# A hybrid GLA and S5 decoder block on one core: half of the S5 rotation on ScalarE, and the late products in another order

## The chip, the cores and the metric

The kernel runs on one core of one Trainium2 chip. The metric is the device time of one execution in microseconds (us), the median of three runs. TensorE (PE) multiplies matrices, VectorE (DVE) and ScalarE (ACT) work on elements, GpSimd (POOL) and SyncE (SP) issue most transfers. Each engine has one queue and works through it in order; semaphores hold an instruction until what it needs is there.

## The reference

One layer on 512 tokens plus 16 meta tokens of width 1024. After a norm, one wide product gives q, k, v, the attention gate r, the S5 input u and two mixing gates z. Attention and S5 run side by side:

```python
proj = rmsnorm(h, g_mix_pre) @ w_in            # q k v r a_low u z_gla z_ssm
o = gla_chunked(q, k, v, log_a)
o = rmsnorm(o, gla_norm_g) * silu(r)
y_gla = o @ w_o_gla
y_s = s5_ssm(u, ...)                            # complex diagonal state, 64 groups of 64 states
glu = gelu(y_s) @ w_glu + b_glu
y_ssm = glu[..., :D] * sigmoid(glu[..., D:])
mixed = sigmoid(z_gla) * y_gla + sigmoid(z_ssm) * y_ssm
h = h + rmsnorm(mixed @ w_out)
h = h + rmsnorm(square(relu(rmsnorm(h) @ w_ff1)) @ w_ff2)
```

In S5 each state is `x_t = L x_(t-1) + B u_t`, `y_t = Re(C x_t) + D u_t` with complex L, B and C.

## The kernel before

**Weights and slots.** Every large product is made with float32 split in two halves: `whi` is the rounded weight, `wlo` the rest, and 24 matmuls per 128 output columns (8 steps of k, three passes: whi with xh, whi with xl, wlo with xh) make one *slot*. For each slot SP loads `wraw` (512 KB), ScalarE makes `whi` (`split_hi`, L161), VectorE makes `wlo` (`split_w_lo`, L176). Each of the three has three buffers, and `slot()` fetches two slots ahead. The list `dense` holds the slots in the order in which PE runs them; `slot()` takes the next.

**What stands between the slots.** The S5 part goes through 8 blocks of 8 groups. In each block, five slots are run with the block's work between them: `turns` (rotation table E by `erot`, loads of U), `kernels` (small matmuls "M,BA" and the row `krow`), the previous block's `output`, `scan`, and the next block's `tables` (M2 and M1). In the first four blocks the slots are the attention's v, k, q and one gate product; `Head` does the attention itself, one block behind for its outputs.

**The late slots**, counted from 0 over the whole list: slots 30 to 33 are gate products z0 to z3, 34 to 41 the attention gate products r0 to r7 (`r_slot`), then z5, o0, o1, o2, z6, o3, o4, z7, o5, o6, o7 (42 to 52), where z is a mixing gate (`gate_slot`) and o an attention output product (`o_slot`). Block 5 has the slots 35 to 39, block 6 the slots 40 to 44, block 7 the slots 45 to 49. An r slot has ScalarE's sigmoid of the product, VectorE's two multiplications (by the product, by the normed attention output `ro`), ScalarE's rounding into `ogh` and VectorE's rest into `ogl`. A z slot has only ScalarE's sigmoid behind it, an o slot only one multiplication by the kept or reloaded gate tile `zt`, which has 4 buffers. All o slots need all of `ogh` and `ogl`.

**The scan.** Real parts lie in partitions 0 to 63, imaginary parts in 64 to 127. `scan` multiplies M1 with U ("U,M"), rotates the result by E, scans along time, and rotates back. A rotation is one product with E's real part over all partitions and, in `turn`, two products with E's imaginary part over 64 partitions each, that read one half of the partitions and write the other, then a sum.

**Order.** A scheduler orders each engine's instructions in the region of the S5 blocks from the program's order and its own estimates; only PE's matmuls keep program order. Instructions keep the order that it found, on every run.

Of the kernel before, what the change touches and what calls it, by code (L numbers as in the profile page):

```python
# [11 lines left out]
AF = mybir.ActivationFunctionType  # L12
# [4 lines left out]
P = 128  # L17
D = 1024
KT = D // P
SEQ = 512  # L20
# [16 lines left out]
T8 = 8  # L37
# [12 lines left out]
def hybrid_block(ctx: ExitStack, tc: tile.TileContext, io, out: bass.AP):  # L50
    nc = tc.nc
    V, S, G = nc.vector, nc.scalar, nc.gpsimd
# [27 lines left out]
    def mk(pool, shape, dt=F32, tag=None, **kw):  # L80
        count[0] += 1
        name = f"{tag or 'x'}_{count[0]}"
        size = 1
        for n in shape[1:]:
            size *= n
        if pool not in lined or size % LINE == 0:
            return pool.tile(shape, dt, tag=tag or name, name=name, **kw)
        t = pool.tile([shape[0], -(-size // LINE) * LINE], dt, tag=tag or name, name=name, **kw)[:, :size]
        if len(shape) == 2:
            return t  # L90
        dims = " ".join("abcd"[: len(shape) - 1])
        return t.rearrange(f"p ({dims}) -> p {dims}", **dict(zip("abcd", shape[1:])))
# [29 lines left out]
    sgn = mk(cst, [P, 1], tag="sgn")  # L122
# [197 lines left out]
    V, S = InOrder(nc.vector), InOrder(nc.scalar)  # L320
# [107 lines left out]
    V, S = nc.vector, nc.scalar  # L428
# [3 lines left out]
    ps = bank()  # L432
# [56 lines left out]
    zg = mk(dr, [KT, P, SEQ], tag="zgd")  # L489
# [35 lines left out]
    def gate_slot(c0, m, dst, tile_of=None):  # L525

        def go(w):
            ps = bank("mm")
            feat_tile(w, xh, xl, 0, SEQ, ps)
            t = tile_of() if tile_of else mk(po_, [P, SEQ], tag="zt", bufs=4)  # L530
            S.activation(by_phase(t), phases(ps), AF.Sigmoid)
            if tile_of:
                nc.gpsimd.dma_start(dst[m], t)
            else:
                kept[m] = t

        dense.append((cols("w_in", c0 + m * P), go))
# [11 lines left out]
    Lr = mk(p5, [P, 9, GRP], tag="Lr")  # L549
    Li = mk(p5, [P, 9, GRP], tag="Li")  # L550
    CA = mk(p5, [P, GRP, HG], tag="CA")
    CB = mk(p5, [P, GRP, HG], tag="CB")
# [5 lines left out]
    behind_norm.__enter__()  # L558
    V.tensor_reduce(i16, ident.rearrange("p (b h) -> p h b", h=HG), axis=mybir.AxisListType.X, op=ALU.add)

# [52 lines left out]
    with tc.issue_after(loaded.ins):  # L613
        for i, name in enumerate(("b_re", "b_im")):
            nc.sync.dma_start(bn[:, i], io[name][0])
        for i, name in enumerate(("c_re", "c_im")):
            src = io[name][0].rearrange("(t g) h n -> (g h) t n", g=GB)
# [119 lines left out]
    def c_rows():  # L737
        for t0 in range(0, NBLK, 4):
            for src, dst, sg_ in ((cnat, CA, True), (cnatx, CB, False)):
                yield  # L740
                ps = bank()
                for t in range(4):
                    PE.transpose(ps[:, t * P : (t + 1) * P], src[:, t0 + t].rearrange("p a n -> p (a n)"), ident)
                d = dst[:, t0 * GB : (t0 + 4) * GB, :].rearrange("p g h -> p (g h)")
                V.tensor_scalar_mul(d, ps, sgn if sg_ else -1.0)

    def b_bar():

# [69 lines left out]
    b5 = pool("b5", stack=sb5, side="right")  # L818
# [154 lines left out]
    class Block:  # L973
# [3 lines left out]
            self.blk = blk  # L977
            self.gs = slice(blk * GB, (blk + 1) * GB)

        def table(self, dst, n, a_, b_, g0):  # L980
            gg = slice(self.blk * GB + g0, self.blk * GB + g0 + 4)
            sh = [P, 4, n, HG]
            d = dst[:, g0 : g0 + 4]
            ta = mk(b5, [P, 4, 9, HG], tag="mta")[:, :, :n]
            lrb = Lr[:, :n, gg].rearrange("p l g -> p g l").unsqueeze(3).to_broadcast(sh)
            lib = Li[:, :n, gg].rearrange("p l g -> p g l").unsqueeze(3).to_broadcast(sh)
            V.tensor_mul(d, a_[:, gg].unsqueeze(2).to_broadcast(sh), lrb)
            V.tensor_mul(ta, b_[:, gg].unsqueeze(2).to_broadcast(sh), lib)
            V.tensor_add(d, d, ta)

        def loads(self, queue=nc.sync):

            self.B = mk(b5, [P, GB, 2, NST_N], tag="B")
# [5 lines left out]
        def tables(self):  # L999

            M1 = self.M1 = mk(b5, [P, GB, 2, NST_N], tag="M1", bufs=1)
            self.M2 = mk(b5, [P, GB, 9, HG], tag="M2", bufs=2)
            B, (lr, li) = self.B, (self.lam[:, i].unsqueeze(2).to_broadcast([P, GB, 2, NST_N]) for i in range(2))
            for g0 in (0, 4):
                self.table(self.M2, 9, CA, CB, g0)
                yield
            V.tensor_mul(M1, B, lr)
            yield
            V.tensor_mul(B, B, li)
            V.tensor_sub(M1[:, :, 0], M1[:, :, 0], B[:, :, 1])  # L1010
            V.tensor_add(M1[:, :, 1], M1[:, :, 1], B[:, :, 0])
            yield
# [26 lines left out]
        def scan(self):  # L1039

            M3 = self.M3 = mk(b5, [P, GB, P], tag="M3", bufs=1)
            for sp in range(T8):
                s = T8 - 1 - sp
                nc.sync.dma_start(M3[sp * HG : (sp + 1) * HG], kpad[self.gs].rearrange("g h l -> h g l")[:, :, 112 - 16 * s : 240 - 16 * s])
            U, E = self.U, self.E
            v, vs = (mk(b5, [P, GB, NST], tag=t, bufs=1) for t in ("v", "vs"))

            def turn(src, gg):

                V.tensor_mul(vs[:64, gg], src[64:], E[64:, 1, gg])  # L1050
                V.tensor_mul(vs[64:, gg], src[:64], E[:64, 1, gg])  # L1051

            for g0 in range(0, GB, 4):
                ps = bank()
                pv = ps[:, : 4 * NST].rearrange("p (g c) -> p g c", g=4)
                for g in range(4):
                    PE.matmul(pv[:, g], self.M1[:, g0 + g].rearrange("p c n -> p (c n)"), U[:, g0 + g, :NST], start=True, stop=True)
                gg = slice(g0, g0 + 4)
                V.tensor_mul(v[:, gg], pv, E[:, 0, gg])
                turn(pv, gg)  # L1060
            V.tensor_sub(v, v, vs)
            flat = v.rearrange("p g c -> p (g c)")
            V.tensor_tensor_scan(flat, d0.rearrange("p g c -> p (g c)"), flat, 0.0, op0=ALU.mult, op1=ALU.add)  # L1063
            X = self.X = mk(b5, [P, GB, NST], tag="X", bufs=1)
            V.tensor_mul(X, v, E[:, 0])
            turn(v, slice(0, GB))
            V.tensor_add(X, X, vs)

        def output(self):

# [2 lines left out]
            for j in range(4):  # L1073
                for part in range(2):
                    for e in range(2):
                        g = 4 * e + j
                        if part:
                            a, b = self.X[:, g, 1:], self.M2[:, g, 1:9, :].rearrange("p l h -> p (l h)")
                        else:
# [30 lines left out]
    def r_slot(m):  # L1110
        def go(w):
            ps = bank("mm")
            feat_tile(w, xh, xl, 0, SEQ, ps)
            o = mk(po_, [P, SEQ], tag="ro", bufs=2)
            nc.sync.dma_start(o, og_dram[m])
            sg_ = mk(po_, [P, SEQ], tag="rs", bufs=2)
            S.activation(sg_, ps, AF.Sigmoid)
            V.tensor_mul(sg_, sg_, ps)
            V.tensor_mul(sg_, sg_, o)  # L1119
            split_hi(ogh[:, m], sg_)  # L1120
            V.tensor_sub(ogl[:, m], sg_, f32(ogh)[:, m])  # L1121

        dense.append((cols("w_in", C_R + m * P), go))

    def o_slot(m):
        def go(w):
            ps = bank("mm")
            feat_tile(w, ogh, ogl, 0, SEQ, ps)
            if m in kept:
                zt = kept.pop(m)  # L1130
            else:
                zt = mk(po_, [P, SEQ], tag="zt", bufs=4)
                nc.sync.dma_start(zt, zg[m])
            V.tensor_mul(by_phase(zt), by_phase(zt), phases(ps))
            nc.gpsimd.dma_start(td[m], zt)

        dense.append((cols("w_o_gla", m * P), go))
# [5 lines left out]
        gate_slot(C_ZS, 4 + h, zs, early_tile)  # L1143
    for m in range(4):
        gate_slot(C_ZG, m, zg, early_tile)
    for m in range(KT):
        r_slot(m)
    for kind, m in (("z", 5), ("o", 0), ("o", 1), ("o", 2), ("z", 6), ("o", 3), ("o", 4), ("z", 7), ("o", 5), ("o", 6), ("o", 7)):
        if kind == "o":
            o_slot(m)  # L1150
        else:
            gate_slot(C_ZG, m, zg)
    blocks[0].loads(nc.gpsimd)
    first = blocks[0].tables()
    for _ in range(4):
# [2 lines left out]
    for b, blk in enumerate(blocks):  # L1158
# [30 lines left out]
        if b == HEADS:  # L1189
# [3 lines left out]
            po_ = pool("po", stack=so, padded=True)  # L1193
# [39 lines left out]
    for c in range(0, D, 256):  # L1233
        ss_ = []
        for i, w in enumerate(load_w(wg[:, D + c : D + c + 256])):
            m = c // P + i
            ps = bank("mm")
# [3 lines left out]
            zt = mk(pgl, [P, SEQ], tag="zi", bufs=2)  # L1241
# [110 lines left out]
    f = mk(pff, [P, MF, SEQ], tag="f")  # L1352
# [44 lines left out]
    for m in range(EARLY, MF):  # L1397
        ps = bank("mm")
# [12 lines left out]
    po_ = pool("pout", side="right", padded=True)  # L1411
# [139 lines left out]
```

## Time and profile before

| | |
|---|---|
| time, median of 3 (lowest to highest) | 911.29 us (910.85 to 911.82) |
| the profiled execution: its time, its span | 912.54 us, 910.8 us |
| DVE busy | 668.6 us, 1182 instructions |
| ACT busy | 403.1 us, 656 instructions |
| S5 blocks 0 to 7 in the trace | from about 113 to 430 us |
| PE's part of the chain that ended last | 85% |

In the timeline a row is one instruction with its start and its duration; the brackets say how long its engine was idle before it and what ended that. An instruction's record overlaps the next one's by some hundredths. In the table by stretches, each engine's column is the time in which it was busy in that stretch, and PEclk is the clock granted to PE, 1.00 being full.

### The profile page before, as it was taken

The page shows a single profiled execution, that of the slowest core. Times are in us where ns is not written, and L with a number is a line of the kernel's source. Part 1 is how long each engine was busy: PE and PEld are TensorE (multiplying, and loading weights), DVE is VectorE, ACT ScalarE, POOL GpSimd, SP SyncE. Part 2 cuts the span into 40 slices and gives each one's busy share as a digit, 9 for nine tenths or more (in the row PEclk, how much of TensorE's full clock was granted, in tenths as well). Part 3 has the DMA queues.
Part 4 walks back from the last instruction along what each step waited for, and adds up shares of the span by engine and source line. Part 5 has one row for each costly group of instructions (what it writes and reads, how often), then busy time and mean ns, then how long its engine had stood idle before and what let it go on. Part 6 is the DMA issues. An engine that isn't in the chain of part 4 may idle for free.

```text
span 910.8 us, 13359 instructions
## 1 busy us (share of the span) xinstructions
PE 885.9 (97%) x4924; PEld 752.6 (83%) x4924; DVE 668.6 (73%) x1182; ACT 403.1 (44%) x656; POOL 92.1 (10%) x165
## 2 busy tenths in 40 slices
PE   8999999999999998699999999999999999999996
PEld 6998899898988787488888888988888888888885
DVE  7899788968787689845544676466866668688786
ACT  6363446556553433222422554333322236665763
POOL 1222100010101201012100000011111110000001
PEclk9999999999999999799999999999999999999999
DMA  7835855555445464747845683369898967856564
GB/s 222 215 110 172 230 137 161 138 139 157 111 149 160 131 146 130 198 124 213 266 144 154 198 214 110 132 199 346 291 336 289 342 238 232 294 190 191 178 208 140
DMA packets 175740, 176.13 MB, mean 193 GB/s; under 512 B 22917, under 2 KB 137673, under 8 KB 175674
## 3 DMA queue, kind: packets, MB, share of 16 engines
q1 hardware_dynamic: 158872, 117.89, 46.1%
q0 software_dynamic: 15632, 53.44, 16.8%
q10 hardware_dynamic: 1170, 3.94, 1.2%
q8 instruction: 39, 0.64, 0.3%
q14 instruction: 27, 0.22, 0.1%
HBM read 139.81 MB, written 35.42 MB: 192 GB/s over the span
## 4 chain that ended last, share of the span: by engine, by line
PE 85%; DVE 9%; DMA 2%; issue 2%; ACT 2%; SPq 0%; DVEq 0%; ACTq 0%
PE mm L60 62%; PE sm L60 20%; PE sm L65 2%; DMA wraw<-in_w_in_dram 1%; DVE wlo L176 1%; DVE mta L236 1%; DVE rs L1119 0%; DVE vs L1050 0%; DVE epb L237 0%; DVE vs L1051 0%; DVE v L1063 0%; DVE b L484 0%; PE mm L65 0%; DVE ogl L1121 0%; DVE mn L482 0%
## 5 line engine op out<-in xcount | busy, mean ns | idle before, releaser
L161 ACT ACTIVATE whi<-wraw 128x1024 fp32r<-128x1024 f32 x101 | 106.9, 1059 | 223.3 <-PE mm L60 196.4
L176 DVE TENSOR_TENSOR wlo<-wraw,whi 128x1024 fp32r<-128x1024 f32 x101 | 123.3, 1222 | 91.2 <-ACT whi L161 91.0
L60 PE MATMUL mm<-xh,whi 128*128 128x512 f32 (+2 forms) x544 | 183.1, 337 | 0.5 <-ACT xh L78 0.5
L60 PE MATMUL mm<-xh,wlo 128*128 128x512 f32 (+2 forms) x544 | 179.6, 330 | 2.8 <-DVE wlo L176 2.7
L60 PE MATMUL mm<-xl,whi 128*128 128x512 f32 (+2 forms) x544 | 179.1, 329 | 0.7 <-DVE xl L78 0.7
L60 PEld LDWEIGHTS mm<-xh,wlo 128*128 128x128 f32 x544 | 103.1, 189 | 12.7 <-DVE wlo L176 3.1
L60 PEld LDWEIGHTS mm<-xh,whi 128*128 128x128 f32 x544 | 103.1, 190 | 11.6 <-issue 1.4
L60 PEld LDWEIGHTS mm<-xl,whi 128*128 128x128 f32 x544 | 103.1, 190 | 9.6 <-DVE xl L78 1.1
L60 PE MATMUL mm<-hh,whi 128*128 128x512 f32 (+1 forms) x280 | 104.0, 371 | 0.0
L60 PE MATMUL mm<-hl,whi 128*128 128x512 f32 (+1 forms) x280 | 103.8, 371 | 0.0
L60 PE MATMUL mm<-hh,wlo 128*128 128x512 f32 (+1 forms) x280 | 103.8, 371 | 0.0
L1428 DVE TENSOR_TENSOR wlo<-wraw,whi 128x1024 fp32r<-128x1024 f32 x56 | 68.4, 1223 | 21.5 <-ACT whi L1424 21.5
L60 PE MATMUL sm<-wlo,fh 128*128 128x512 f32 x192 | 74.8, 390 | 0.0
L60 PE MATMUL sm<-whi,fl 128*128 128x512 f32 x192 | 74.7, 389 | 0.0
L60 PE MATMUL sm<-whi,fh 128*128 128x512 f32 x192 | 74.7, 389 | 0.0
L1424 ACT ACTIVATE whi<-wraw 128x1024 fp32r<-128x1024 f32 x56 | 58.7, 1049 | 18.5 <-PE mm L60 11.7
L60 PEld LDWEIGHTS mm<-hl,whi 128*128 128x128 f32 x280 | 52.7, 188 | 9.1
L60 PEld LDWEIGHTS mm<-hh,whi 128*128 128x128 f32 x280 | 52.7, 188 | 9.1
L60 PEld LDWEIGHTS mm<-hh,wlo 128*128 128x128 f32 x280 | 52.7, 188 | 9.0
L60 PE MATMUL mm<-gh,whi 128*128 128x512 f32 x128 | 49.8, 389 | 0.0
L60 PE MATMUL mm<-gl,whi 128*128 128x512 f32 x128 | 49.8, 389 | 0.0
L60 PE MATMUL mm<-gh,wlo 128*128 128x512 f32 x128 | 49.8, 389 | 0.0
(424 smaller groups left out, 1590.5 us busy)
## 6 DMA issues: line engine op xcount, KB each, us to landing
wraw<-in_w_ff_dram SPq DMA_DIRECT2D x56, 512.0 KB
wraw<-in_w_in_dram SPq DMA_DIRECT2D x48, 512.0 KB
w2raw<-in_w_ff_dram POOLq DMA_DIRECT2D x16, 1024.0 KB, 8.5
t2d<-w2t POOLq DMA_DIRECT2D x16, 1024.0 KB, 6.0
wraw<-t2d SPq DMA_DIRECT2D x32, 512.0 KB
wraw<-in_w_glu_dram SPq DMA_DIRECT2D x16, 512.0 KB
M<-kpad SPq DMA_DIRECT2D x64, 64.0 KB
wraw<-in_w_o_gla_dram SPq DMA_DIRECT2D x8, 512.0 KB
```

What stands on the lines that cost most here:

```text
L60: ins = nc.tensor.matmul(*args, **kw)
L65: ins = nc.tensor.transpose(*args, **kw)
L161: S.activation(dst, src, AF.Copy, scale=scale)
L176: V.tensor_sub(lo, raw, f32(hi))
L236: V.tensor_mul(ta, E[:, :, :, 1 : m + 1], br)
L1424: halved = S.activation(bh, raw, AF.Copy)
L1428: V.tensor_sub(bl, raw, f32(bh))
```

## The change

Three edits.

1. **Rotation.** `turn` becomes `exchanged`: ScalarE copies the lower partitions to the upper and the other way round (four copies of 64x260 out of PSUM and two of 64x520 per block), and VectorE then multiplies `vs` once by E's imaginary part over all 128 partitions. Signs move from one sum to the other.
2. **Tables.** M2's part for power 0 is a copy by ScalarE. The rest is one VectorE product over all 8 groups (128x1024) and two products and two sums over 4 groups (128x512), where there were three instructions of 128x576 for each half. The scaling of CA and CB (four instructions in `c_rows`) goes from VectorE to ScalarE.
3. **Slots.** The late slots run in the order r0, r1, z5, r2, r3, z6, r4, r5, r6, r7, z7, o0 to o7. `zt` has 6 buffers.

```diff
@@ gate_slot, o_slot @@
-            zt = mk(po_, [P, SEQ], tag="zt", bufs=4)
+            zt = mk(po_, [P, SEQ], tag="zt", bufs=6)
@@ c_rows @@
-                V.tensor_scalar_mul(d, ps, sgn if sg_ else -1.0)
+                S.activation(d, ps, AF.Copy, scale=sgn if sg_ else -1.0)
@@ Block.tables (table is removed) @@
-            V.tensor_mul(d, a_[:, gg].unsqueeze(2).to_broadcast(sh), lrb)
-            V.tensor_mul(ta, b_[:, gg].unsqueeze(2).to_broadcast(sh), lib)
-            V.tensor_add(d, d, ta)
...
+            S.copy(self.M2[:, :, 0], CA[:, self.gs])
...
+            V.tensor_mul(self.M2[:, :, 1:], ca, lrb)
             for g0 in (0, 4):
-                self.table(self.M2, 9, CA, CB, g0)
+                gg = slice(g0, g0 + 4)
+                ta = mk(b5, [P, 4, T8, HG], tag="mta")
+                V.tensor_mul(ta, cb[:, gg], lib[:, gg])
+                V.tensor_add(self.M2[:, gg, 1:], self.M2[:, gg, 1:], ta)
                 yield
@@ Block.scan @@
-            def turn(src, gg):
-
-                V.tensor_mul(vs[:64, gg], src[64:], E[64:, 1, gg])
-                V.tensor_mul(vs[64:, gg], src[:64], E[:64, 1, gg])
+            def exchanged(src, gg):
+
+                S.copy(vs[:64, gg], src[64:])
+                S.copy(vs[64:, gg], src[:64])
...
                 V.tensor_mul(v[:, gg], pv, E[:, 0, gg])
-                turn(pv, gg)
-            V.tensor_sub(v, v, vs)
+                exchanged(pv, gg)
+            V.tensor_mul(vs, vs, E[:, 1])
+            V.tensor_add(v, v, vs)
...
+            exchanged(v, slice(0, GB))
             V.tensor_mul(X, v, E[:, 0])
-            turn(v, slice(0, GB))
-            V.tensor_add(X, X, vs)
+            V.tensor_mul(vs, vs, E[:, 1])
+            V.tensor_sub(X, X, vs)
@@ the list of slots @@
-    for m in range(KT):
-        r_slot(m)
-    for kind, m in (("z", 5), ("o", 0), ("o", 1), ("o", 2), ("z", 6), ("o", 3), ("o", 4), ("z", 7), ("o", 5), ("o", 6), ("o", 7)):
...
+    for kind in ("r0", "r1", "z5", "r2", "r3", "z6", "r4", "r5", "r6", "r7", "z7", *(f"o{m}" for m in range(KT))):
...
```

The order of instructions shows what slot 44 waits for. On VectorE, between the last rotation of block 6 and the low half for slot 44, the program before has block 7's rotation table (mta, epb, E), its table M1 (M, B), and then the low half of o1 (`wlo_4233`):

```order
L236 TENSOR_TENSOR mta_4375<-E_4352 128x512
L237 TENSOR_TENSOR epb_4376<-E_4352 128x512
L238 TENSOR_TENSOR E_4352<-mta_4375,epb_4376 128x8x32
L239 TENSOR_TENSOR E_4352<-mta_4375,epb_4376 128x8x32
L1007 TENSOR_TENSOR M_752_4223<-B_4218,lam_4219 128x1024
L1009 TENSOR_TENSOR B_4218<-B_4218,lam_4219 128x1024
L1010 TENSOR_TENSOR M_752_4223<-M_752_4223,B_4218 128x8x64
L1011 TENSOR_TENSOR M_752_4223<-M_752_4223,B_4218 128x8x64
L176 TENSOR_TENSOR wlo_4233<-wraw_4229,whi_4231 128x1024
```

The program of the change has, at the same place, the product of r7 (`rs_4307`) among the same rows, and the low half of z7 (`wlo_4236`) at their end:

```order
L236 TENSOR_TENSOR mta_4385<-E_4362 128x512
L1117 TENSOR_TENSOR rs_4307<-rs_4307,mm_4280 128x512
L237 TENSOR_TENSOR epb_4386<-E_4362 128x512
L238 TENSOR_TENSOR E_4362<-mta_4385,epb_4386 128x8x32
L239 TENSOR_TENSOR E_4362<-mta_4385,epb_4386 128x8x32
L1004 TENSOR_TENSOR M_750_4225<-B_4220,lam_4221 128x1024
L1006 TENSOR_TENSOR B_4220<-B_4220,lam_4221 128x1024
L1007 TENSOR_TENSOR M_750_4225<-M_750_4225,B_4220 128x8x64
L1008 TENSOR_TENSOR M_750_4225<-M_750_4225,B_4220 128x8x64
L176 TENSOR_TENSOR wlo_4236<-wraw_4232,whi_4234 128x1024
L1118 TENSOR_TENSOR rs_4265<-rs_4265,ro_4263 128x512
```

So slot 44's low half has kept its place behind block 7's tables, and one product has joined the rows ahead of it. On ScalarE, at the same place, the program before has the sigmoid of r7 (`rs_4178`), the high half of o0, the roundings of r6 and r7, the sigmoid of z5 (`zt`), block 7's copies d and E and the high half of o1 (`whi_4231`):

```order
L1117 ACTIVATE rs_4178<-mm_4151 128x512
L161 ACTIVATE whi_4147<-wraw_4145 128x1024
L161 ACTIVATE ogh_3657<-rs_4102 128x512
L161 ACTIVATE ogh_3657<-rs_4178 128x512
L531 ACTIVATE zt_4260<-mm_4235 128x512
L1016 COPY d_217_1237<-prm_489 128x8x64
L1018 COPY E_4352<-E_88_491 128x16x9
L161 ACTIVATE whi_4231<-wraw_4229 128x1024
```

The program of the change has the sigmoid of r6 (`rs_4265`), the two exchanging copies of the scanned state (`vs` from `v`), d and E, the sigmoid of r7 (`rs_4307`) and the high half of z7 (`whi_4234`):

```order
L1116 ACTIVATE rs_4265<-mm_4238 128x512
L1047 COPY vs_4194<-v_4193 64x520
L1048 COPY vs_4194<-v_4193 64x520
L1013 COPY d_217_1237<-prm_489 128x8x64
L1015 COPY E_4362<-E_88_491 128x16x9
L1116 ACTIVATE rs_4307<-mm_4280 128x512
L161 ACTIVATE whi_4234<-wraw_4232 128x1024
```

Slot 44's high half has moved behind the sigmoid of slot 43, where before it stood behind the sigmoid of slot 42 only.

More of the change, by code (lines that the diff above doesn't have):

```diff
@@ L529, in go @@
             feat_tile(w, xh, xl, 0, SEQ, ps)
-            t = tile_of() if tile_of else mk(po_, [P, SEQ], tag="zt", bufs=4)
+            t = tile_of() if tile_of else mk(po_, [P, SEQ], tag="zt", bufs=6)
             S.activation(by_phase(t), phases(ps), AF.Sigmoid)
@@ L978, in __init__ @@
             self.gs = slice(blk * GB, (blk + 1) * GB)
[L980 to L987, printed above, removed]
-            V.tensor_mul(ta, b_[:, gg].unsqueeze(2).to_broadcast(sh), lib)
-            V.tensor_add(d, d, ta)
         def loads(self, queue=nc.sync):
@@ L1003, in tables @@
             B, (lr, li) = self.B, (self.lam[:, i].unsqueeze(2).to_broadcast([P, GB, 2, NST_N]) for i in range(2))
+            sh = [P, GB, T8, HG]
+            S.copy(self.M2[:, :, 0], CA[:, self.gs])
+            lrb, lib = (L[:, 1:, self.gs].rearrange("p l g -> p g l").unsqueeze(3).to_broadcast(sh) for L in (Lr, Li))
+            ca, cb = (C[:, self.gs].unsqueeze(2).to_broadcast(sh) for C in (CA, CB))
+            V.tensor_mul(self.M2[:, :, 1:], ca, lrb)
             for g0 in (0, 4):
-                self.table(self.M2, 9, CA, CB, g0)
+                gg = slice(g0, g0 + 4)
+                ta = mk(b5, [P, 4, T8, HG], tag="mta")
+                V.tensor_mul(ta, cb[:, gg], lib[:, gg])
+                V.tensor_add(self.M2[:, gg, 1:], self.M2[:, gg, 1:], ta)
                 yield
@@ L1145, in hybrid_block @@
         gate_slot(C_ZG, m, zg, early_tile)
-    for m in range(KT):
-        r_slot(m)
-    for kind, m in (("z", 5), ("o", 0), ("o", 1), ("o", 2), ("z", 6), ("o", 3), ("o", 4), ("z", 7), ("o", 5), ("o", 6), ("o", 7)):
-        if kind == "o":
-            o_slot(m)
+    for kind in ("r0", "r1", "z5", "r2", "r3", "z6", "r4", "r5", "r6", "r7", "z7", *(f"o{m}" for m in range(KT))):
+        m = int(kind[1])
+        if kind[0] == "z":
+            gate_slot(C_ZG, m, zg)
         else:
-            gate_slot(C_ZG, m, zg)
+            (r_slot if kind[0] == "r" else o_slot)(m)
     blocks[0].loads(nc.gpsimd)
```

## The prediction

> **What bounds the kernel now.** I read the page's busy shares first, then what PE waited for, then the stretches around the waits, then the rows at the waits.
>
> ```profile
> PE 885.9 (97%) x4924; PEld 752.6 (83%) x4924; DVE 668.6 (73%) x1182; ACT 403.1 (44%) x656; POOL 92.1 (10%) x165
> PE mm L60 <- DVE wlo L176: 8.2, 2, 5.5
> PE mm L60 <- ACT whi L161: 2.6, 1, 2.6
> PE sm L65 <- DVE CA L745: 1.6, 1, 1.6
> PE sm L65 <- ACT on L961: 0.5, 1, 0.5
> 340.00:360.00 20.00, 18.15 (x127) 14.78 (x125) 19.79 (x37) 7.72 (x13) 2.98 (x5) 1.00 0.50 137
> 360.00:380.00 20.00, 12.78 (x48) 9.86 (x48) 19.48 (x35) 5.99 (x8) 0.00 (x0) 0.85 0.78 182
> 380.00:400.00 20.00, 18.35 (x106) 14.72 (x107) 6.37 (x9) 1.92 (x4) 4.11 (x7) 0.81 0.35 110
> ```
>
> PE is busy 97% of the span, so VectorE's 73% is worth nothing as a mean. What can be won are PE's waits and its slow stretches. In the middle of the kernel the waits are 8.2, 2.6, 1.6 and 0.5 us (the second number is how often, the third the longest). The first two lie in 340 to 400, the one stretch where VectorE has no idle time (third busy column, 19.79 and 19.48 of 20) and where PEclk falls.
>
> ```profile
> 357.44 0.47 PE L60 MATMUL mm<-xh,whi 128*128 128x512 f32 x1
> 360.82 0.80 PE L60 MATMUL mm<-xh,wlo 128*128 128x512 f32 x1 [2.66 <-DVE wlo L176]
> 375.42 0.50 PE L60 MATMUL mm<-ogh,whi 128*128 128x512 f32 x1 [2.56 <-ACT whi L161]
> 381.65 0.80 PE L60 MATMUL mm<-ogh,wlo 128*128 128x512 f32 x1 [5.49 <-DVE wlo L176]
> 361.00:363.50 2.50, 2.50 (x6) 1.97 (x7) 2.50 (x4) 0.63 (x1) 0.00 (x0) 0.50 0.46 110
> 384.00:387.50 3.50, 3.50 (x10) 2.73 (x9) 0.46 (x1) 0.00 (x0) 0.00 (x0) 0.50 1.05 340
> 304.11 5.48 PE mm L60 x24
> ```
>
> Slot 42 (z5) starts at 357.44 and waits 2.66 us for its low half. Slot 44 (o1) waits 2.56 us for its high half and 5.49 us for its low half. After both low halves PE runs at clock 0.50: from 360.8 to 363.5, and from 381.65 to about 387.4, which costs half of that, 1.35 and 2.9 us. A slot at full clock takes 5.48 us (24 matmuls). So this region loses 2.66 + 2.56 + 5.49 + 1.35 + 2.9 = 15.0 us, and that is the most the change can win here.
>
> **What the edits cost on the engines.**
>
> ```profile
> L1050 DVE TENSOR_TENSOR vs<-sm,E 64x260 f32<-64x260 f32 x16 | 6.9, 430 | 0.3
> L1050 DVE TENSOR_TENSOR vs<-v,E 64x520 f32<-64x520 f32 x8 | 5.6, 696 | 0.1
> L1067 DVE TENSOR_TENSOR X<-X,vs 128x520 f32<-128x520 f32 x8 | 5.6, 696 | 0.1
> L987 DVE TENSOR_TENSOR M<-CA,Lr 128x576 f32<-128x576 f32 x16 | 12.0, 750 | 0.0
> L1007 DVE TENSOR_TENSOR M<-B,lam 128x1024 f32<-128x1024 f32 x8 | 9.8, 1220 | 3.6 <-DMA lam<-lamd 3.6
> L1118 DVE TENSOR_TENSOR rs<-rs,mm 128x512 f32<-128x512 f32 x8 | 5.5, 683 | 5.6 <-ACT rs L1117 5.6
> L842 ACT COPY vt<-mm 128x256 f32<-128x256 f32 x8 | 2.9, 364 | 6.4 <-PE mm L60 6.3
> L1016 ACT COPY d<-prm 128x512 f32<-128x512 f32 x8 | 4.9, 617 | 8.8 <-DVE v L1063 8.8
> L767 ACT COPY BA<-sm 128x512 f32<-128x512 f32 x2 | 2.0, 1118 | 0.0
> ```
>
> Rotation, per block on VectorE: four of 0.43 and two of 0.70 go (3.1 us), two of 0.70 come (1.4). Tables: six of 0.75 go (4.5), one of 1.22 and four of 0.69 come (4.0). VectorE sheds 1.7 + 0.5 = 2.2 us per block. ScalarE gets four copies of 64x260 and two of 64x520. Before shows no copy of ScalarE from one half of the partitions to the other. The nearest rows are its copies of 256 and of 512 elements, 0.36 and 0.62 us; its dearest copy of 512 is BA's, 1.12; and nothing at all is the other end. I take 0.37 and 0.62, since the work per partition is the same. That adds about 2.7 us per block to an engine that is busy 44%.
>
> Slots: an r slot costs VectorE a low half of 1.22 and three rows of about 0.69, 3.3 us; a z slot 1.22. Before, block 5 holds five r slots, 16.4 us; after, three r and two z, 12.3. With the 2.2 us, block 5 loses 6.3 us of VectorE's work. That is the load that makes the backlog of 340 to 380.
>
> **Slot 42 is r6 after the change.** Its low half stands behind r4's product, the output of block 5 and block 6's tables. r4 ends where r6 ended before, with the last row ahead of this one:
>
> ```profile
> 347.66 0.66 PE L60 MATMUL sm<-M,BA 128*32 128x128 f32 x16
> L1117 ACT ACTIVATE rs<-mm 128x512 f32<-128x512 f32 x8 | 4.7, 581 | 3.7 <-PE mm L60 3.7
> L1035 DVE COPY_PREDICATED krow<-odd,sm 128x128 f32<-128x128 int32 x8 | 2.4, 297 | 6.2 <-ACT krow L1034 6.2
> 354.54 0.23 DVE L1036 SCALAR_TENSOR_TENSOR krow<-i,vecs,krow 128x16 f32<-128x16 f32 x1
> ```
>
> Sigmoid 0.58 to 348.3; then on VectorE r4's product, krow (0.30 and 0.23), the table product 1.22, four table rows of 0.69, two output rows of 0.68, r4's second product, the low half 1.22: 8.4 us, 356.7, and about 0.5 for the wait for ScalarE's square of the output. 357.2 is before slot 42's first matmul at 357.44. I take the 2.66 and the 1.35 as gone. VectorE must come to r4 without a backlog, which the 6.3 us give it; if a backlog of 1 us is left, PE waits about 1 us here.
>
> **Slot 44 is z7, and here a wait stays.** The low half keeps its place behind block 7's tables (the order above). r6 now runs unstalled, 357.44 + 5.48 = 362.9. Sigmoid 0.58, to 363.5.
>
> ```profile
> 355.74 1.90 PE L60 MATMUL sm<-U,M 128*128 128x65 f32 x16
> L161 ACT ACTIVATE ogh<-rs 128x512 fp32r<-128x512 f32 x8 | 5.1, 633 | 15.9 <-DVE rs L1119 15.9
> L1063 DVE TENSOR_TENSOR_SCAN v<-d,v 128x520 f32<-128x520 f32 x8 | 9.9, 1236 | 0.1
> ```
>
> The scan of block 6 ends at the same time: r5 ends where U,M begins, 355.7; sigmoid, r5's product, a low half and r5's second product, 0.58 + 0.68 + 1.22 + 0.69, to 358.9; on ScalarE the rounding and four copies, 0.63 + 1.46, to 361.0; `vs`, the sum and the scan, 0.7 + 0.7 + 1.24, to 363.6. Then two exchanging copies, 1.24, to 364.8; the product `vs` and the difference X, 1.4, to 366.2. Behind them comes a stretch that the trace of before has whole:
>
> ```profile
> 372.40 0.28 DVE L236 TENSOR_TENSOR mta<-E 128x128 f32<-128x128 f32 x1
> ...
> 380.38 1.22 DVE L176 TENSOR_TENSOR wlo<-wraw,whi 128x1024 fp32r<-128x1024 f32 x1
> ```
>
> From the first row's start to the last row's end 9.2 us, and r7's product in it, 0.68. The low half is there at 366.2 + 9.9 = 376.1, against 381.6 before: **5.5 us won**, in which slot 42's 2.66 + 1.35 are contained. PE still idles: r7 ends at 368.4, so that z7 waits some 7 us in all, first for its high half (behind r7's sigmoid, 0.58, and its own 1.06), then for the low half.
>
> **After the wait** the clock will be low again. The two stretches at 0.50 were 2.7 and 5.75 us long; I take their mean, 4.2, a loss of 2.1 in place of 2.9: **0.8 won**; the ends are none (2.9 won) and as before (0). The Trainium skill, page "TensorE: Matmul & The Clock Gate", Part 1, says that full clock comes back after about 3.4 us of sustained work; by that the loss would be 1.7 and the forecast 0.4 lower. The row at 384 to 387.5, still at 0.50 more than 2.4 us after the restart, fits it only up to 385; here the trace's 5.75 decides.
>
> **The two small waits.**
>
> ```profile
> 302.25 1.86 PE L65 MATMUL sm<-ident,on 128*128 128x128 f32 x8 [0.52 <-ACT on L961]
> 254.67 1.05 ACT L161 ACTIVATE whi<-wraw 128x1024 fp32r<-128x1024 f32 x1
> ```
>
> `on` needs VectorE's chain of small rows, which comes after the scan and the rotation back. With block 4's 2.2 us fewer in front it should come 1 us or more sooner: **0.5 won**. The wait for CA stays: ScalarE's scaling comes behind the sigmoid there, at about the time at which VectorE did it. I count 0, with 0.3 either way.
>
> **Sum:** 5.5 + 0.8 + 0.5 = 6.8 us. The profiled execution took 912.54 us and would take 905.7; the median of 911.29 becomes **904.5**. PE's work after 400 has no gap that could take this back.
>
> **The rivals.**
>
> *The whole loss goes.* If the scan's copies and block 7's tables did not hold z7's low half, all 15.0 and the 0.5 would go: 895.8. For it speaks VectorE's lighter load, against it the order on VectorE: nine rows of block 7 are ahead of that low half, and they can't begin before r6's sigmoid and the copies.
>
> *Nothing is won, because a transfer comes last.* z7's raw weight is loaded behind block 6's M and block 7's B and lam.
>
> ```profile
> 356.99 3.63 SPq L1044 DMA_DIRECT2D M<-kpad  x8
> 374.31 1.06 ACT L161 ACTIVATE whi<-wraw 128x1024 fp32r<-128x1024 f32 x1 [2.20 <-DMA wraw<-in_w_o_gla_dram]
> ```
>
> Before, from M's first issue to the landing there are 17.3 us. krow comes at 348.3 + 0.68 + 0.53 = 349.5 instead of 354.8, 5.3 us sooner, M's issue at 351.7, the landing at 369.0. With 1.06 for the high half that is 370.1, and VectorE does not reach the low half before 374.9: about 5 us of cover. A landing past 374 takes the gain back one for one, past 380 all of it: 911.
>
> *Slower, by `on` in blocks 1 to 4.* PE's transposes of `on` have next to no slack (0.52 us of wait in block 4). ScalarE now has to copy the scanned state before VectorE goes on to the chain that ends in `on`. Each us that this comes later costs PE one us in each of four blocks. Against it: in the queues, the rows removed between U,M and that chain are worth more than 2 us. To end 1.8 us slower than now, the chain must lose 6.8 + 1.8 = 8.6, or 2.2 us per block, and so be over 3 us later than I count, which needs copies three to four times as dear as assumed: 913 to 916. In the same queue a high half (254.67, block 2) stands behind the copies; its slot starts over 7 us later, so that it does not decide.
>
> **How the numbers follow.** The forecast has 0.79, the whole loss gone 0.08, nothing won 0.08, slower 0.05. Within the forecast: copies for nothing take 1.2 off and full clock after the wait 2.1, 901.2, and 0.7 for the small waits, 900.5. Upward, copies at BA's price add 1.0 at the two long ones and 0.8 at the four short ones, the long slow clock 0.8, a late r6 1.0 and `on` as before 0.5: 908.6. With a part of the case in which the transfer takes most of it, the range is 900.5 to 909.5. A measurement of this kernel tells about 0.2%, 1.8 us, from no change. Faster by more than that: 0.79 + 0.08 = 0.87; within it 0.08; slower 0.05.
>
> **What would show it.** In the profile after, no wait at slot 42 (r6); one wait pair at z7 of 6 to 8 us in sum, whi first and wlo behind it, with VectorE busy without a gap from r6's sigmoid to z7's low half; a stretch at clock 0.50 behind it; no wait for `on`; the 64x520 copy at about 0.62 us. I am wrong if z7's low half is early, if PE waits in blocks 0 to 4, or if a raw weight is the last to come.

## The result and the profile after

The changed kernel takes **905.16 us** (median of 4 runs, 904.78 to 905.83) beside 911.56 us (910.85 to 912.92) for the kernel before in the same job: ratio **0.9929**, 95% interval 0.9912 to 0.9946. The forecast was 904.5. The profiled execution took 905.44 us with a span of 903.7, against 912.54 and 910.8 before.

The busy shares on the page of the changed kernel:

```profile
PE 883.1 (98%) x4924; PEld 752.1 (83%) x4924; DVE 647.2 (72%) x1138; ACT 428.6 (47%) x716; POOL 92.1 (10%) x165
```

What its PE waited for (in total, how often, the longest):

```profile
PE mm L60 <- DVE wlo L176: 5.2, 1, 5.2
...
PE mm L60 <- ACT whi L161: 2.0, 1, 2.0
PE sm L65 <- ACT CA L745: 1.7, 1, 1.7
```

And its stretches around the waits (the columns are PE, PEld, DVE, ACT and POOL busy, PEclk, share of DMA, GB/s):

```profile
340.00:360.00 20.00, 20.00 (x136) 16.64 (x135) 14.93 (x26) 8.50 (x16) 2.98 (x5) 1.00 0.38 91
360.00:380.00 20.00, 12.76 (x46) 9.53 (x45) 19.32 (x31) 7.78 (x12) 0.00 (x0) 0.74 0.77 185
```

VectorE's load in 340 to 360 falls from 19.79 to 14.93 us, and PE has no gap there any more. One pair of waits is left, at z7; the wait for `on` has left the list. To see where the 7.1 us of span come from, a list of waits isn't enough, since PE also loses time without waiting (a lower clock, matmuls that trail another engine). So I compare the times of the same PE instructions in both timelines. Before, then after:

```profile
120.50 1.89 PE L60 MATMUL sm<-U,M 128*128 128x65 f32 x16
...
395.57 0.66 PE L60 MATMUL sm<-M,BA 128*32 128x128 f32 x16
```

```profile
121.44 1.89 PE L60 MATMUL sm<-U,M 128*128 128x65 f32 x16
...
354.20 1.90 PE L60 MATMUL sm<-U,M 128*128 128x65 f32 x16
...
388.48 0.67 PE L60 MATMUL sm<-M,BA 128*32 128x128 f32 x16
```

The first row is "U,M" of block 0, the second of the three after is "U,M" of block 6 (355.74 before, in the prediction), the last "M,BA" of block 7. That divides the span:

| stretch | before | after | won |
|---|---|---|---|
| start to U,M of block 0 | 120.50 | 121.44 | -0.94 |
| to U,M of block 6 (blocks 0 to 5) | 235.24 | 232.76 | 2.48 |
| to M,BA of block 7 (slots 42 to 44) | 39.83 | 34.28 | 5.55 |
| to the end | 515.2 | 515.2 | 0.0 |

The forecast had 6.3 us for the third row (5.5 and 0.8), 0.5 for the second and nothing for the first. PE's rows of the third stretch:

```profile
355.90 0.47 PE L60 MATMUL mm<-xh,whi 128*128 128x512 f32 x1
...
369.12 0.68 PE L60 MATMUL mm<-xh,whi 128*128 128x512 f32 x1 [2.05 <-ACT whi L161]
...
375.42 0.80 PE L60 MATMUL mm<-xh,wlo 128*128 128x512 f32 x1 [5.19 <-DVE wlo L176]
...
379.00 0.63 PE L60 MATMUL mm<-xl,whi 128*128 128x512 f32 x1
379.43 0.44 PE L60 MATMUL mm<-xh,wlo 128*128 128x512 f32 x1
```

r6 runs through from 355.90. z7 waits 2.05 and 5.19 us, and then has matmuls of 0.63 up to 379.00 and of 0.44 and less from 379.43: 4.0 us at half clock, where o1 before had 5.75. The clock is down already ahead of the second wait: the row at 369.12 takes 0.68.

### The profile page after: what moved, and what is told of

Read it like the earlier page. It is cut to its first block, busy times and chain, and to the rows that moved or that the text cites. A ratio compares the mean times of both kernels' runs of the same rounds, so it can differ in the third digit from the quotient of the medians.

```text
span 903.7 us, 13365 instructions
## 1 busy us (share of the span) xinstructions
PE 883.1 (98%) x4924; PEld 752.1 (83%) x4924; DVE 647.2 (72%) x1138; ACT 428.6 (47%) x716; POOL 92.1 (10%) x165
## 4 chain that ended last, share of the span: by engine, by line
PE 94%; DVE 2%; ACT 1%; issue 1%; DMA 1%; SPq 0%; POOL 0%; DVEq 0%; ACTq 0%; POOLq 0%
PE mm L60 69%; PE sm L60 22%; PE sm L65 2%; PE mm L65 0%; SPq L1041 0%; DMA M<-kpad 0%; DVE c L1489 0%; POOL qd L1107 0%; DMA kpad<-krow 0%; DMA grow<-in_g_mix_pre_dram 0%; ACT xh L78 0%; ACT vs L1048 0%; ACT vs L1047 0%; DVE c L1483 0%; DVE mta L236 0%
## 5 line engine op out<-in xcount | busy, mean ns | idle before, releaser
L161 ACT ACTIVATE fh<-f 128x512 fp32r<-128x512 f32 x48 | 30.3, 631 | 44.5 <-PE sm L60 29.4
```

Source lines behind the costliest of these rows:

```text
L161: S.activation(dst, src, AF.Copy, scale=scale)
```

## The experiments

Each is the kernel named with one edit, timed beside the kernel before on the same chip (its medians: 912.49 for the two halves alone, the tables behind and the early weight; 912.38 for the exchange and the tables back and for the last two below; 911.97 for CA and the doubled copies). "Stretch", in the profiled execution, is U,M of block 6 to M,BA of block 7: 39.83 us before, 34.28 after.

### The two halves of the change alone

The S5 edits alone are the change without its third edit, the order alone is nothing but that edit. Against the changed kernel and against the kernel before:

```diff
-    for kind in ("r0", "r1", "z5", "r2", "r3", "z6", ...):
+    for m in range(KT):
+        r_slot(m)
+    for kind, m in (("z", 5), ("o", 0), ("o", 1), ...):
```

```diff
-    for m in range(KT):
-        r_slot(m)
-    for kind, m in (("z", 5), ("o", 0), ("o", 1), ...):
+    for kind in ("r0", "r1", "z5", "r2", "r3", "z6", ...):
```

> The edits of the S5 part alone (ScalarE's exchange, the shorter tables, the CA scaling on ScalarE), the slots in the old order. My theory: what sets the time is how many VectorE rows stand ahead of the low halves of slots 42 and 44, and the block's 2.2 us count once at slot 42 and twice at slot 44, less about 1.7 us in which VectorE waits for the copies; the wait for on goes as in the changed kernel (1.3 us). Slot 42's wait 0.5 to 2.7 us, slot 44's low half about 2.7 us sooner than 380.4 + 1.2, so 2.7 to 4 us faster than before: about 908. Rival, that the lighter work carries the change: 5 us or more faster, 906 or less. Rival, that the work does not matter at all and only the order does: within 1 us of before.

Measured: **906.86 us** (906.5 to 908.48), ratio 0.9942 [0.9923, 0.9962]; stretch 36.03.

> The slot order alone (gate products between the attention gates, output products last), VectorE's old rotation, tables and scaling. My theory: r6's low half is in time, so slot 42's 2.66 us and its slow stretch go; z7's low half comes about 2.0 us later than in the changed kernel (1.5 us since all up to r6 is later, 0.5 us since the old rotation is as long as the copies with their waits, or a little longer), 377.4, so about 5 us faster than before, 906.5; the wait for on stays at 0.5 us. Rival, that the lighter work carries the change: 2 us or less faster, 909 or more. If the two edits add up, this run's gain and that of the S5 edits alone sum to about 6.4 us; if they take the same waits away, to more than that.

Measured: **909.27 us** (907.75 to 909.93), ratio 0.9961 [0.9948, 0.9974]; stretch 36.52. PE's waits in 350 to 380 in the timeline, the S5 edits alone, then the order alone (with one row of VectorE):

```profile
356.29 0.50 PE L60 MATMUL mm<-xh,wlo 128*128 128x512 f32 x1 [0.24 <-DVE wlo L176]
...
370.00 0.50 PE L60 MATMUL mm<-ogh,whi 128*128 128x512 f32 x1 [3.00 <-ACT whi L161]
...
375.95 0.80 PE L60 MATMUL mm<-ogh,wlo 128*128 128x512 f32 x1 [5.22 <-DVE wlo L176]
```

```profile
362.59 0.76 DVE L989 TENSOR_TENSOR M<-M,mta 128x576 f32<-128x576 f32 x1
...
370.23 0.50 PE L60 MATMUL mm<-xh,whi 128*128 128x512 f32 x1 [1.69 <-ACT whi L161]
...
378.34 0.80 PE L60 MATMUL mm<-xh,wlo 128*128 128x512 f32 x1 [7.38 <-DVE wlo L176]
```

My theory gave the larger part to the order, and that was wrong: the S5 edits alone win 5.6 us, the order alone 3.2 (from 912.49). Their sum, 8.8, is above the 6.4 us that both bring (911.56 to 905.16). In the stretch it is 3.80 and 3.31, 7.1 in sum, against 5.55 for both. The medians alone leave this difference within the noise of the three ratios; the stretch shows where it comes from. Each of them alone takes nearly all of slot 42's wait away (0.24 us left with the S5 edits, none with the order), and that can be won only once. Neither makes the waits at slot 44 shorter: 8.05 us before, 8.22 with the S5 edits, 9.07 with the order. With the order alone PE comes to slot 44 (z7) 4.2 us sooner after U,M of block 6 than before, and the low half ends only 3.2 us sooner; VectorE is still doing a row of the old tables in the middle of the rotation (first line, 0.76 us).

### Parts of the S5 edits put back

The exchange alone, and then the tables alone, as before:

```diff
-                S.copy(vs[:64, gg], src[64:])
-                S.copy(vs[64:, gg], src[:64])
+                V.tensor_mul(vs[:64, gg], src[64:], E[64:, 1, gg])
+                V.tensor_mul(vs[64:, gg], src[:64], E[:64, 1, gg])
...
-            V.tensor_mul(vs, vs, E[:, 1])
```

> The changed kernel with the exchange back on VectorE (four products of 64x260 and two of 64x520 for each block, no copies on ScalarE); the tables, the CA scaling and the slot order as changed. My theory: on the path from block 6's U,M to z7's low half the copies with their waits (0.9 and 0.2 us idle) are nearly as long as the products they replace, so that the exchange is worth about 0.7 us there, and up to 1.3 us at on: 905.9 to 907.2. Rival, the exchange carries the change: 908 or more. Rival, the copies cost as much as they save: within 0.5 us of 905.2.

Measured: **909.07 us** (907.89 to 909.67), ratio 0.9964 [0.9950, 0.9978]; stretch 35.52.

```diff
-            S.copy(self.M2[:, :, 0], CA[:, self.gs])
...
-            V.tensor_mul(self.M2[:, :, 1:], ca, lrb)
             for g0 in (0, 4):
...
+                self.table(self.M2, 9, CA, CB, g0)
```

> The changed kernel with the old tables (twelve products of 576 elements in halves, nothing of them on ScalarE); the exchange, the CA scaling and the slot order as changed. My theory: VectorE has 3.5 us of slack before r4's product, and the tables' 0.5 us stand behind it only in part: 905.2 to 906. Rival, the tables carry the change: 907 or more.

Measured: **907.00 us** (905.99 to 908.08), ratio 0.9944 [0.9930, 0.9958]; stretch 35.90.

The rival was right on the exchange: without it the time is 3.9 us above the changed kernel's (3.2 by the ratios, since each job has its own runs of before). Without the tables it is 1.8 above, at the edge of the rival's range and not in mine, but 1.4 by the ratios, which is within their noise; in the profiles the stretch is 1.62 longer. Of the exchange's part 1.24 us lie in the stretch (0.7 expected) and 2.45 in blocks 0 to 5, at `on`. Who waited for `on` (line 961) before, and in the kernel with the exchange back; after the change the same view has no row there:

```profile
  PEld sm L65: 2.4, 8
  PE sm L65: 0.5, 1
```

```profile
  PEld sm L65: 2.3, 7
  PE sm L65: 0.5, 1
```

The loss was not one wait of 0.5 us but 2.4 us: weight loads of the transposes, waiting in four blocks for one piece of `on` after the other. That doesn't show as idle time of PE. It shows as a longer group. The one of block 4, with 1.86 us in the prediction's row at 302.25, is this after the change:

```profile
301.54 1.03 PE L65 MATMUL sm<-ident,on 128*128 128x128 f32 x8
```

In blocks 1 to 4 these groups take 1.29, 1.42, 1.42 and 1.86 us before and 1.03 to 1.04 after; with the wait of 0.52 that makes 2.36 of the 2.48 us won in blocks 0 to 5. The tables alone, put back, leave these groups at 1.03 and 1.04.

### CA scaled on VectorE again

```diff
-                S.activation(d, ps, AF.Copy, scale=sgn if sg_ else -1.0)
+                V.tensor_scalar_mul(d, ps, sgn if sg_ else -1.0)
```

> The changed kernel with CA and CB scaled on VectorE again, all else as changed. My theory: the wait for CA falls from 1.67 to about 1.55 us, and the slow stretch of about 4 us behind that wait, which some executions show and some do not (0.58 in 86 to 90 in the changed kernel's profile, 1.00 in that of the kernel with the work edits alone, at the same wait of 1.67), does not hang on which engine scales: 904 to 906. Rival, the longer wait on ScalarE brings the slow stretch, which costs 1.5 us: 903.7 or less, and no execution with it.

Measured: **904.98 us** (904.67 to 905.50), ratio 0.9920 [0.9906, 0.9934]. The stretch 86 to 90 of three kernels (changed; S5 edits alone; changed with CA on VectorE):

```profile
86.00:90.00 4.00, 4.00 (x12) 3.15 (x11) 0.00 (x0) 0.74 (x2) 2.77 (x7) 0.58 1.08 294
```

```profile
86.00:90.00 4.00, 4.00 (x25) 3.30 (x23) 0.00 (x0) 1.79 (x4) 1.91 (x6) 1.00 1.10 318
```

```profile
86.00:90.00 4.00, 4.00 (x12) 3.10 (x12) 2.98 (x4) 0.17 (x1) 2.77 (x7) 0.58 0.70 173
```

The wait in front of it, in the changed kernel and in the one with CA on VectorE (with the S5 edits alone it is 1.67 too):

```profile
84.33 0.64 PE L65 MATMUL sm<-ident,Lr 64*64 64x64 f32 x8 [1.67 <-ACT CA L745]
```

```profile
84.32 0.63 PE L65 MATMUL sm<-ident,Lr 64*64 64x64 f32 x8 [1.59 <-DVE CA L745]
```

The low clock (0.58) comes once behind ScalarE's scaling and once behind VectorE's, and it stays away once behind ScalarE's at the same wait. So it does not hang on the engine that scales, as expected. Of the twelve profiles seven have it and five do not; the last section shows what divides them. In the changed kernel's profile it lengthens the time from the transposes behind that wait to U,M of block 0: 37.1 us, against 35.6 before and 35.5 with the S5 edits alone, 1.5 us. That is the -0.94 of the table above (the wait itself came 0.5 us sooner): it belongs to the execution, not to the edit. How many of the changed kernel's other three executions have it is not known: their spans are 903.0 to 904.0, none of them 1.5 below the profiled one's 903.7.

### The copies made twice

```diff
-                S.copy(vs[:64, gg], src[64:])
-                S.copy(vs[64:, gg], src[:64])
+                for _ in range(2):
+                    S.copy(vs[:64, gg], src[64:])
+                    S.copy(vs[64:, gg], src[:64])
```

> The changed kernel with each of ScalarE's exchanging copies made twice (2.7 us more on ScalarE for each block; the second writes what the first wrote). My theory: the copies are on the path at two places of a block, so their price counts in full. z7's low half comes 2.0 to 2.7 us later. on, which in the changed kernel is ready 2.3, 1.6, 1.6 and 0.2 us before PE turns it in blocks 1 to 4, comes 2.0 to 2.7 us later, so PE waits up to 0.4, 1.1, 1.1 and 2.5 us and its transposes trail ScalarE again (0.25, 0.4, 0.4, 0.8 us): 4 to 7 us. Together 910 to 915, the time of the kernel before or more. Rival, the copies are hidden by ScalarE's idle time: 905 to 906.5. Rival, only the path to z7 feels them: 907 to 908.

Measured: **908.54 us** (908.36 to 909.93), ratio 0.9963 [0.9951, 0.9976]; stretch 37.24. The second rival came closest, 0.5 us short. In its timeline the first row is the last small one of `on`'s chain in block 4, the second PE's turning of `on`; the other two, of VectorE, stand on the path to z7, which restarts at 377.86, 2.4 us later:

```profile
296.72 0.16 DVE L158 SCALAR_TENSOR_TENSOR ors<-orr_a,ors 128x4 f32<-128x4 f32 x1
...
301.58 1.03 PE L65 MATMUL sm<-ident,on 128*128 128x128 f32 x8
...
361.76 0.70 DVE L1059 TENSOR_TENSOR vs<-vs,E 128x520 f32<-128x520 f32 x1 [2.47 <-ACT vs L1049]
...
367.65 0.70 DVE L1066 TENSOR_TENSOR vs<-vs,E 128x520 f32<-128x520 f32 x1 [1.96 <-ACT vs L1049]
```

The waits for the copies grow from 0.88 and 0.21 to 2.47 and 1.96 us. But PE turns `on` at 301.58, as at 301.54 without the extra copies. In the order found for this kernel the small rows of `on`'s chain stand in VectorE's idle time, ahead of block 5's rotation rows: the last of them starts at 296.72, where the changed kernel has it 2.8 us later:

```profile
299.54 0.15 DVE L158 SCALAR_TENSOR_TENSOR ors<-orr_a,ors 128x4 f32<-128x4 f32 x1
```

So the rival of the prediction, slower because later copies make `on` later, finds no support: a copy twice as dear does not touch `on`, in an order that is found anew for it. With the order held, no run tried it.

### What is left at z7

In the next four, edits on top of the changed kernel. First only the place of four VectorE rows:

```diff
-            V.tensor_mul(M1, B, lr)
+            with tc.issue_after(low44[0].ins) if self.blk == 7 else ExitStack():
+                V.tensor_mul(M1, B, lr)
```

(and the same for the three rows that complete M1; `low44` is z7's low half.)

> The changed kernel with block 7's four M1 rows (3.85 us on VectorE) behind z7's low half rather than ahead of it. My theory, VectorE's order sets z7's restart: the low half ends at about 372.2 rather than 375.4, z7's wait for it falls from 5.2 to about 2.0 us, the wait for the high half stays at 2.0, and the output products behind it find their weights in time: about 902. Rival, something else comes last at z7 (the raw weight, the high half): 905, no change. Rival, the wait goes to the next slot, because M1's rows now stand ahead of o0's low half: 903.5 to 905.

Measured: **901.73 us** (901.63 to 902.26), ratio 0.9885 [0.9866, 0.9904]; stretch 31.01.

```profile
369.03 0.51 PE L60 MATMUL mm<-xh,whi 128*128 128x512 f32 x1 [1.85 <-ACT whi L162]
...
372.41 0.80 PE L60 MATMUL mm<-xh,wlo 128*128 128x512 f32 x1 [2.45 <-DVE wlo L177]
```

The wait falls from 5.19 to 2.45 us and the time by 3.4, to the 902 expected, with no other edit. VectorE's order sets z7's restart. Next, only the transfer: z7's raw weight (slot 44) is issued in slot 41, ahead of block 6's M.

```diff
+        if n == 41:
+            early[44] = raw_w(dense[44][0])[1]
```

> The changed kernel with z7's raw weight loaded one slot earlier, ahead of block 6's M, B and lam; its halves are then made before block 6's scan and block 7's rows. My theory: z7 starts right behind r7 with no wait (2.05 + 5.19 us of wait and 1.9 us of slow clock gone), but o0's halves now stand where z7's stood (behind z7's sigmoid on ScalarE and behind block 7's rows on VectorE), so that o0 waits 4 to 5 us and the clock falls there: 901 to 903. Rival, nothing takes the wait's place: 896. Rival, the earlier load delays block 6's M or another transfer and that becomes the wait: 904 or more.

Measured: **903.05 us** (902.65 to 904.12), ratio 0.9898 [0.9881, 0.9916]; stretch 30.50.

```profile
375.88 0.50 PE L60 MATMUL mm<-ogh,whi 128*128 128x512 f32 x1 [3.58 <-ACT whi L161]
...
377.22 0.50 PE L60 MATMUL mm<-ogh,wlo 128*128 128x512 f32 x1 [0.60 <-DVE wlo L176]
...
396.27 0.50 PE L60 MATMUL mm<-ogh,wlo 128*128 128x512 f32 x1 [1.73 <-DVE wlo L176]
```

z7 has no wait, and the wait stands at the next slot, o0, as expected (4.2 us in two parts), with a new one of 1.73 behind "U,M" of block 7. Now both, and the order on ScalarE too: block 7's M1 behind o0's low half, and z7's sigmoid and the copy of block 5's transposed output behind o0's high half.

```diff
+        if n == 41:
+            early[44] = raw_w(dense[44][0])[1]
...
-            V.tensor_mul(M1, B, lr)
+            with tc.issue_after(low45[0].ins) if self.blk == 7 else ExitStack():
+                V.tensor_mul(M1, B, lr)
...
-            S.activation(by_phase(t), phases(ps), AF.Sigmoid)
+            with tc.issue_after(hi45[0].ins) if dst is zg and m == 7 else ExitStack():
+                S.activation(by_phase(t), phases(ps), AF.Sigmoid)
```

> The changed kernel with z7's raw weight loaded one slot earlier, block 7's M1 rows behind o0's low half, and ScalarE's high half for o0 ahead of z7's sigmoid. My theory, the loss at z7 and what came in its place at o0 is the order on VectorE and ScalarE and nothing else: z7 starts without a wait, and o0's low half, with no M1 row ahead of it, comes about 1 us late: 897 to 899. Rival, the wait moves on again (to o1, or to U,M of block 7 behind M1): 900 to 902.5. Rival, without a VectorE or ScalarE row in front a transfer is the last to come at o0: 901 or more.

Measured: **900.60 us** (898.69 to 901.95), ratio 0.9871 [0.9854, 0.9889]; stretch 28.27. The waits at o0 are 1.18 and 0.78 us, and 1.73 behind "U,M" of block 7 stays: the first rival (900 to 902.5), the wait that moves on, was right, and not my 897 to 899. Last, o0's raw weight one slot sooner as well, and the rotations of block 7 behind o0's low half, the rest of M1 behind o1's (`behind(n)` queues rows after the low half of slot n):

```diff
+        if n in (41, 42):
+            early[n + 3] = raw_w(dense[n + 3][0])[1]
...
-            V.tensor_mul(B, B, li)
+            with behind(46) if self.blk == 7 else ExitStack():
+                V.tensor_mul(B, B, li)
...
-                erot(self.E, n, n, b5)
+            with behind(45) if self.blk == 7 else ExitStack():
+                for n in (8, 16, 32):
+                    erot(self.E, n, n, b5)
```

> The changed kernel with the raw weights of z7 and o0 loaded one slot earlier and all of block 7's rows (the rotations, M1) behind the low halves of o0 and o1. My theory: no wait at z7 and none at o0, so the whole of the loss left in the changed kernel, 2.05 + 5.19 + 1.9 = 9.1 us, goes: 896 to 897. Rival, the rows put back make PE wait at U,M of block 7 or for krow: 899 to 903. Rival, the transfers come last: 900 or more.

Measured: **898.51 us** (897.58 to 899.36), ratio **0.9853** [0.9833, 0.9872]; stretch 24.18. This is the fastest of all, 6.7 us below the changed kernel, between my 896 to 897 and the 899 of the rival. Neither z7 nor o0 waits. Of the 9.1 us about 2.1 come back, as waits behind "U,M" of block 7:

```profile
389.42 0.50 PE L60 MATMUL mm<-ogh,whi 128*128 128x512 f32 x1 [1.54 <-ACT whi L173]
...
390.68 0.50 PE L60 MATMUL mm<-ogh,wlo 128*128 128x512 f32 x1 [0.54 <-DVE wlo L178]
```

## Why the prediction came out right, step by step

The time was off by 0.7 us. The mechanism at slots 42 and 44 was right. That the sum came so close is luck: three terms were off and cancelled, and the size of a fourth, the clock, was right by chance.

**Slot 42: right.** r6 starts at 355.90 and its low half ends at 354.8 (353.60 + 1.22), with 1.1 us to spare. VectorE does come to r4 without a backlog: it is idle for 3.47 us ahead of r4's product.

```profile
346.92 0.69 DVE L1117 TENSOR_TENSOR rs<-rs,mm 128x512 f32<-128x512 f32 x1 [3.47 <-ACT rs L1116]
...
353.60 1.22 DVE L176 TENSOR_TENSOR wlo<-wraw,whi 128x1024 fp32r<-128x1024 f32 x1
```

**Slot 44: the mechanism right, the size 0.8 us too good.** The order on VectorE was as said, one pair of waits stays (7.2 us, "6 to 8"), and the experiment with M1 behind confirms what holds it. Counted from r6's start I had the restart 18.7 us later (376.1 against 357.44), and it is 19.5 (375.42 against 355.90). The step that failed is the chain to the scan: I had the scan's end 6.2 us after r6's start (363.6), and it is 6.9 (362.84).

```profile
357.89 0.63 ACT L161 ACTIVATE ogh<-rs 128x512 fp32r<-128x512 f32 x1 [1.89 <-DVE rs L1118]
...
358.55 0.37 ACT L1047 COPY vs<-sm 64x260 f32<-64x260 f32 x1
...
359.73 0.37 ACT L1048 COPY vs<-sm 64x260 f32<-64x260 f32 x1
...
360.13 0.70 DVE L1058 TENSOR_TENSOR vs<-vs,E 128x520 f32<-128x520 f32 x1 [0.88 <-ACT vs L1048]
...
361.60 1.24 DVE L1061 TENSOR_TENSOR_SCAN v<-d,v 128x520 f32<-128x520 f32 x1
```

Durations were right: the copies take 0.37 and 0.63 us (0.37 and 0.62 taken). What I left out is the time between engines. The rounding starts at 357.89, 2.0 us after r6's start, where the sum of durations in front of it has 1.5; each start stands some hundredths to three tenths behind the end that released it.

**The clock behind the wait: the size right, by chance.** From z7's restart to the transposes behind the slot it is 7.04 us (375.42 to 382.46), from o1's before 7.91 (381.65 to 389.56): 0.87 won, 0.8 forecast. But the low clock does not begin at the restart, as the forecast counted it, and it is as long after (first) as before (second):

```profile
369.29:379.51 10.22, 5.03 (x12) 3.44 (x13) 10.12 (x14) 3.24 (x4) 0.00 (x0) 0.50 0.63 168
```

```profile
377.39:387.61 10.22, 5.96 (x14) 4.71 (x15) 7.00 (x8) 1.06 (x1) 0.55 (x1) 0.50 0.65 184
```

Both stretches last 10.24 us (their edges lie just outside these windows). What PE loses by them depends on where its restart falls: 6.1 us had passed at the restart after, 4.3 before. The mean of two unlike stretches, which the forecast took, does not contain that.

**`on`: 0.5 forecast, 2.4 won.** The step that failed was to take the loss from the list of waits. The rest of it was in the length of the transposes, and a look at who waits for `on` would have shown 2.4 before.

**CA: the edit right, the execution not.** The wait changes by 0.1 us and the edit by nothing that can be measured; the profiled execution lost 1.5 us behind it to a low clock, which belongs to no edit.

So in span: 5.5 + 0.8 + 0.5 = 6.8 forecast; 4.7 + 0.87 in the stretch, 2.5 in the blocks before and -0.9 at the start, 7.1, measured. In medians of several runs, 6.4 with the run beside it.

**The rivals.** *The whole loss goes* did not occur. Its "nine rows of block 7" are only the end of the queue: sixteen rows of block 7 stand ahead of that low half, and the 9.2 us of the sum hold all of them. The loss does not go by itself; it takes edits at three engines, as the last experiment above shows, and even then 2 us come back. *A transfer comes last*: z7's raw weight held its high half only to 368.01 (369.0 forecast), 5.1 us before VectorE came to the low half, so it was hidden as said; with the weight early the wait only moves. *Slower by `on`* did not occur: `on` comes sooner, and copies made twice did not delay it in the order found for them.

```profile
368.01 1.06 ACT L161 ACTIVATE whi<-wraw 128x1024 fp32r<-128x1024 f32 x1 [0.31 <-DMA wraw<-in_w_in_dram]
...
374.15 1.22 DVE L176 TENSOR_TENSOR wlo<-wraw,whi 128x1024 fp32r<-128x1024 f32 x1
```

## What to carry to other kernels

Read a loss at a handover from "who waited for this tile", weight loads included, and from the length of the group: PE can lose 2.4 us where its list of waits shows 0.5. Two edits that each remove the same wait don't add up, so time each alone and both together. Once a wait is known to hang on an engine's order, move the rows that nobody needs soon behind the ones that PE needs: four rows moved here brought 3.4 us, and the early transfer alone brought less, since the next slot inherits the wait.

## What the hardware showed that I had not expected

**The low clock comes in whole windows.** In the twelve profiles there are nineteen stretches at half clock ahead of the kernel's last products. They last 3.41, 6.83, 10.24 or 13.65 us, one to four times 3.41, and within one execution all their ends lie on one grid with steps of 3.41: in the changed kernel's at 85.97, 89.39, 369.28 and 379.52 us. Where the grid lies differs from execution to execution. The Trainium skill, page "TensorE: Matmul & The Clock Gate", Part 1, speaks of an activity window of about 3.4 us that runs freely; these traces agree.

**So the same wait can cost clock or not.** The wait for CA, about 1.6 us in all twelve, is followed by a slow window in the seven profiles in which 1.4 us or more of it lie within one window, and by none in the five in which the grid splits it so that no window has more than 1.25. The changed kernel, and then the S5 edits alone: the window in which the wait ends and the one behind it (PE is busy for 1.74 of 3.41 us in the first, for 2.50 of 3.40 in the second):

```profile
82.56:85.97 3.41, 1.74 (x20) 1.45 (x20) 2.06 (x4) 3.40 (x7) 0.54 (x1) 1.00 0.53 154
85.98:89.38 3.40, 3.40 (x10) 2.64 (x9) 0.00 (x0) 0.76 (x2) 2.34 (x7) 0.50 1.09 309
```

```profile
84.48:87.88 3.40, 2.50 (x22) 2.19 (x23) 1.20 (x2) 3.31 (x7) 0.54 (x1) 1.00 0.81 245
87.88:91.30 3.42, 3.42 (x16) 2.82 (x15) 0.00 (x0) 0.00 (x0) 2.77 (x7) 1.00 1.05 253
```

From 30 us on, a window at full clock with 2.0 us or more of idle PE was always followed by half clock, and one with at most 1.25 never; between 1.4 and 1.9 both occur, and these runs do not say why. The section "HAM oscillation — how this bites in real kernels" of that page of the Trainium skill warns of idle gaps over about 3.4 us; here 2.05 us at z7's high half were enough.

**The clock comes back only at the end of a window.** A window at half clock was the last one when PE was idle in it for at most 0.5 us; with 0.86 us or more another followed. That is why the slow matmuls behind a restart last 4.0 us in one kernel and 5.75 in another. Part 1 of that page of the Trainium skill has full clock back after about 3.4 us of sustained work; these traces agree where the work is counted by whole windows.

**ScalarE moves data between halves of the partitions at the price of a plain copy**: 0.37 us for 64x260 and 0.63 for 64x520, beside 0.36 for 128x256 and 0.62 for 128x512.
